# A decoder block on one core: the feed-forward phase put into program order on all engines, its reloads and stores moved

## Chip, core, metric

The kernel runs on one core of a Trainium2 chip. Five engines take part: TensorE (PE, with its weight loads as a row of their own, PEld), VectorE (DVE), ScalarE (ACT), GpSimd (POOL) and SyncE (SP); SP and POOL start the DMAs here. Each engine runs its own list of instructions in order, and waits at an instruction until what it needs from other engines and DMAs is there. The metric is the device time of one execution in microseconds.

## The reference

One layer of a decoder block on 512 tokens of width 2048, all in float32:

```python
h = rmsnorm(x, attn_norm_g)
c_q, c_kv, k_rope, u_pool, gate_logits = split(h @ w_in)
# multi-scale causal pooling of u_pool, latent attention of c_q, c_kv, k_rope
mixed = g_pool * y_pool + g_attn * y_attn
x = x + mixed @ w_out
h2 = rmsnorm(x, ffn_norm_g)
x = x + (silu(h2 @ w_ffn_gate) * (h2 @ w_ffn_up)) @ w_ffn_down
```

w_ffn_gate and w_ffn_up are 2048 x 5632, w_ffn_down is 5632 x 2048. The last two lines are the feed-forward, the only part that the change touches.

## The kernel before

**Accuracy by splitting.** Every float32 operand is used as the sum of two: "hi", a copy rounded to the format in which TensorE is fast (a cast on ACT, L179), and "lo", the rest (a subtraction on DVE, L180: source minus hi). `split` holds both lines. DVE's L180 always waits for ACT's L179 of the same tile.

**Two phases.** The first 1296 us hold the attention and the output projection; they are emitted by a program of their own and the change leaves them alone. The feed-forward follows. It has three kinds of work.

*Blocks* (class `Macro`) compute a 2 x 2 arrangement of products with seven matrix products in place of eight (the scheme of Strassen and Winograd), in the order 1, 5, 6, 2, 7, 3, 4. A product is 8 matmuls of 128x128 by 128x512 with hi (L1090) and 8 by 128x256 with lo (L1093), added into one PSUM bank. Each block loads five weight tiles of 512 KB by SP (L1067), "11", "s1", "12", "s3" and "22"; "s1" and "s3" are sums of two blocks, whose second half is added by an accumulating DMA on POOL (L1069), which waits for the landing of the first half. `prepare(i)` splits the weights of product i: 1 reads "11", 5 "s1", 6 the sum "s1" + "11" written over "11" (DVE, L1075), 2 "12", 7 "s3", 3 the sum "12" + "11" written over "12" (L1077), 4 "22". The split goes into one of five buffers `ws`. `post(i)` works on the result: 1 copies its bank negated into the bank of 6 (ACT), 5 copies its bank to `p5` (ACT, L1108), 6 copies its bank negated into that of 3 (ACT, L1111), 2 and 4 fold a bank into the result tile `gu` (ACT L1099, DVE L1100), 7 adds `p5` to its bank (`w`, DVE L1117), 3 subtracts `p5` from its bank and adds both parts of `w` into `gu` (L1120, L1121). There are two buffers `gu`, one `p5` and one `w`.

- 44 `GateUp` blocks, one for each 128 rows of the hidden layer. They multiply the gate part by the norm's factor (L1151, after product 3), take silu (ACT, L1152), multiply by the up part (L1154, after product 4) and store the 256 KB product to `F_d` in DRAM (SP, L1155).
- 8 `Down` blocks for each half c of the hidden layer. For c = 0 the result is added to `X2_d` in DRAM by an accumulating DMA on POOL (L1174); for c = 1 the block reloads its part of `X2_d` (SP), adds it (L1168) and stores `out` (SP, L1176 after product 3, L1178 after product 4).

*Plain groups* (class `Plain`), 4 ahead of each half of the `Down` blocks, multiply the first 6 of a half's 22 tiles of `F_d` in three passes (24 matmuls a step, 12 steps). Their activations, tiles "ff", are reloaded from `F_d` by POOL and split by `make_act`. At a group's end two results `gu` are added to `X2_d` by POOL (L1213).

*Operands* (class `Operands`): beside the plain groups the other 16 tiles of `F_d` are reloaded by POOL ("t" and "b") and combined on DVE (`difference`, `sums`, with temporaries "d" and "e" in the buffers of `w` and `gu`) and split into the 28 tiles T that the `Down` blocks multiply. The T, raw weight, ff, t, b and xr tiles share a pool of 36 slots.

**What sets the order.** A list of steps (one product of a block, or one step of a plain group) is walked once (L1329 on). At step n the loop first issues the loads that step n + 3 needs and two more, and `prepare` of step n + 3, then the matmuls of step n, then `post` of step n, then what `extra` holds for n (the reloads and operand parts, distributed by `spread`). Only PE keeps that order on its instruction list (L141, `manual_schedule`); the lists of ACT, DVE, POOL and SP are ordered by a scheduler that works from its own estimate of times. A tile's buffer is given back when the last instruction on it is done; one that waits for a buffer waits at its place in its engine's list.

Of the kernel before, what the change touches and what calls it, by code (L numbers as in the profile page):

```python
# [136 lines left out]
def hybrid_block(ctx, tc, xT, pos, wcq, wckv, wkr, wu, wgp, wga, wgrp, wpo, wq, wkv, wao, wo,  # L137
                 wg, wup, wdp, wds, vec, rgain, ident_d, mask_d, freq_d, cnt_d, out):
    nc = tc.nc
    act, dve, pool, pe = nc.scalar, nc.vector, nc.gpsimd, nc.tensor  # L140
# [12 lines left out]
    def slot(dt=F32, name="s"):  # L153
        return slots.tile([128, 2, 512], dt, name=name, tag="s")
# [4 lines left out]
    def tmp(w=512):  # L159
        return work.tile([128, 528], F32, name="tmp", tag="tmp", bufs=6)[:, :w]  # L160
# [15 lines left out]
    def split(hi, lo, src, scale=None):  # L176

        if scale is None:
            act.copy(out=hi, in_=src)  # L179
            dve.tensor_tensor(out=lo, in0=src, in1=hi.bitcast(F32), op=ALU.subtract)  # L180
        else:
            act.activation(out=hi, in_=src, func=AF.Copy, scale=scale)  # L182
            dve.scalar_tensor_tensor(out=lo, in0=src, scalar=scale, in1=hi.bitcast(F32),
                                     op0=ALU.mult, op1=ALU.subtract)
# [103 lines left out]
    def token_sums(o, acc, tag):  # L288

        box = []  # L290

        def run():
            box.append(ps(tag))
            for t in range(NT):
                pe.matmul(box[0][:, 2 * t:2 * t + 2], acc[:, t * 128:(t + 1) * 128], ones[:, 0:2],
                          start=True, stop=True)

        def post():
            dve.tensor_copy(o, box[0][:, 0:2 * NT].rearrange("p (t two) -> p t two", two=2)[:, :, 0])
        return run, post  # L300
# [702 lines left out]
    class Operands:  # L1003
# [9 lines left out]

        def sums(self):
            t, b, d = self.t, self.b, self.d
            e = self.e = self.temp("e")
            dve.tensor_tensor(out=d[:, :, HI], in0=b[:, :, HI], in1=d[:, :, LO], op=ALU.subtract)
            dve.tensor_tensor(out=e[:, :, LO], in0=t[:, :, HI], in1=b[:, :, HI], op=ALU.subtract)
            dve.tensor_tensor(out=e[:, :, HI], in0=b[:, :, LO], in1=d[:, :, HI], op=ALU.subtract)

        def part(self, i):
            src = {1: (self.t, LO), 2: (self.b, LO), 3: (self.b, HI), 5: (self.d, LO)}
            if i in (4, 6, 7):
                src.update({6: (self.d, HI), 7: (self.e, LO), 4: (self.e, HI)})
            r = slot(F32R, "T")
            split(r[:, :, LO], r[:, :, HI], src[i][0][:, :, src[i][1]])
            self.T[i, self.j] = r

        def steps(self):
            return [self.difference, lambda: self.part(1), lambda: self.part(5), self.sums] + \  # L1030
                [lambda i=i: self.part(i) for i in (2, 6, 7, 3, 4)]

    def slot_temp(name):
        return slot(F32, name)
# [5 lines left out]
    acts = {}  # L1040

    def load_acts(dst, f):
        pool.dma_start(dst, F_d[f])

    def make_act(f):
        r = slot(F32R, "ff")
        load_acts(r[:, 1, :].bitcast(F32), f)
        split(r[:, 0, :], r[:, 1, :], r[:, 1, :].bitcast(F32))
        acts[f] = r

    class Macro:

# [73 lines left out]
    fast = [None]  # L1126

    def wide(name):
        return fast[0].tile([128, 2, 512], F32, name=name, tag="w", bufs=1)

    def wide2(name):
        return wide(name) if name == "d" else fast[0].tile([128, 2, 512], F32, name=name, tag="gu", bufs=2)

    def split_unit(src, early=False):

        if early:
            h, l = (slot(F32R, "ws0").rearrange("p a n -> p (a n)") for _ in range(2))
        else:
            r = fast[0].tile([128, 2, 1024], F32R, name="ws", tag="ws", bufs=WS_BUFS)
            h, l = r[:, 0, :], r[:, 1, :]  # L1140
        split(h, l, src)
        return h, l

    class GateUp(Macro):
# [4 lines left out]
        def done(self, i, g):  # L1149
            if i == 3:  # L1150
                dve.tensor_tensor(out=g[:, 0, :], in0=g[:, 0, :], in1=inv2_bc, op=ALU.mult)  # L1151
                act.activation(out=g[:, 0, :], in_=g[:, 0, :], func=AF.Silu)  # L1152
            elif i == 4:
                dve.tensor_tensor(out=g[:, 1, :], in0=g[:, 0, :], in1=g[:, 1, :], op=ALU.mult)  # L1154
                nc.sync.dma_start(F_d[self.f], g[:, 1, :])  # L1155

    class Down(Macro):

# [5 lines left out]
        def done(self, i, g):  # L1164
            if i == 1 and self.last:
                self.x = slot(F32, "xr")
                nc.sync.dma_start(self.x, X2_d[2 * self.j:2 * self.j + 2].rearrange("a p n -> p a n"))
            for a, c in {2: ((0, LO),), 3: ((0, HI), (1, HI)), 4: ((1, LO),)}.get(i, ()):  # L1168
                dve.tensor_tensor(out=g[:, a, c], in0=g[:, a, c], in1=inv2_bc[:, c], op=ALU.mult)
                if self.last:  # L1170
                    dve.tensor_tensor(out=g[:, a, c], in0=g[:, a, c], in1=self.x[:, a, c], op=ALU.add)
            k = 2 * self.j
            if i == 4 and not self.last:
                pool.dma_start(X2_d[k:k + 2].rearrange("a p n -> p a n"), g, accum_op=ALU.add)  # L1174
            elif i == 4:
                nc.sync.dma_start(out[k + 1], g[:, 1, :])  # L1176
            elif i == 3 and self.last:
                nc.sync.dma_start(out[k], g[:, 0, :])  # L1178

    class Plain:  # L1180
# [24 lines left out]
        def post(self, u):  # L1205
            if u < self.nu - 1:
                return
            for a in range(2):
                o = fast[0].tile([128, 2, 512], F32, name="gu", tag="gu", bufs=2)
                for b in range(2):  # L1210
                    dve.tensor_tensor(out=o[:, b, :], in0=self.acc[2 * a + b], in1=inv2_bc, op=ALU.mult)  # L1211
                k = 4 * self.j + 2 * a
                pool.dma_start(X2_d[k:k + 2].rearrange("a p n -> p a n"), o, accum_op=ALU.add)  # L1213

    macros = [GateUp(f) for f in range(FT)]

# [58 lines left out]

    phase = ExitStack()
    fast[0] = phase.enter_context(tc.tile_pool(name="fast", bufs=1, reuse_waits="tile"))

    sums_run, sums_post = token_sums(t42, xacc2[0], "a")
    bc2_prepare, bc2_run = token_bc(inv2_bc, inv2, "a", lambda: fast[0].tile([128, 512], F32, name="dg", tag="gu", bufs=2))  # L1280

    loads, steps, extra = [], [], {}
# [7 lines left out]
    def add_plain(m):  # L1290
        for u in range(m.nu):
            loads.append((m, u))
            steps.append((m, u, len(loads)))

    def spread(first, count, work):

        for n, f in enumerate(work):
            extra.setdefault(first + n * count // len(work), []).append(f)

    def operand_work(key, f0):  # L1300

        r = []
        for j in range(4):
            o = Operands(key, j, None, None, wide2)

            def fetch(o=o, j=j):
                o.t, o.b = slot(F32, "t"), slot(F32, "b")
                for a in range(2):
                    load_acts(o.t[:, a, :], f0 + 2 * j + a)
                    load_acts(o.b[:, a, :], f0 + 8 + 2 * j + a)  # L1310
            r += [fetch] + o.steps()
        return r

    for m in macros:
        add_macro(m)
# [1 line left out]
                  3: [bc2_prepare], 4: [bc2_run]})  # L1317
    for c in range(2):
        f0 = HT * c
        spread(len(steps) - 6, 6, [lambda f=f: make_act(f) for f in range(f0, f0 + 6)])  # L1320
        n = len(steps)
        for j in range(4):
            add_plain(Plain(wdp[c], j, f0, 3, SETS[j % 2]))
        spread(n, 12, operand_work(c, f0 + 6))
        for j in range(8):
            add_macro(Down(c, wds[c], j, c == 1))

    nload, nprep = 2, 2
    for n, (m, i, _) in enumerate(steps):  # L1329
        while nprep < min(len(steps), n + LEAD + 1):  # L1330
            mm, ii, need = steps[nprep]
            while nload < min(len(loads), need + 2):
                loads[nload][0].load(loads[nload][1])
                nload += 1
            mm.prepare(ii)
            nprep += 1
        m.product(i)
        m.post(i)
        for f in extra.get(n, ()):
            f()  # L1340
    phase.close()


# [73 lines left out]
```

## Time and profile before

| | us |
|---|---|
| median of 3 runs | 2649.8 |
| the three runs | 2646.56, 2649.8, 2650.21 |
| the profiled execution | 2645.02 |
| its span, first to last instruction | 2643.0 |
| first phase, gate and up blocks, plain and down | to 1296, to 2126, to 2643 |

The mean granted TensorE clock of the profiled execution is 0.995 of full speed.

How to read the rows of the profile: an instruction row has its start in us, the duration of one, the engine, the line of the kernel, the operation, out<-in by tile names, the tile's shape and type, how many followed directly, and in brackets how long the engine had been idle before it and what it waited for ("<-DVE w L1117": an operation of DVE at L1117 that wrote or read w). "SPq" and "POOLq" are the moments at which a queue gets a DMA. A DMA row has out<-in, the queue, the count, the size of one and the median time from issue to landing. L1090 stands for line 1090 of the kernel before.

### The profile page before, as it was taken

What the parts mean: (1) busy time and instruction counts of PE and PEld (TensorE: products, weight loads), DVE (VectorE), ACT (ScalarE), POOL (GpSimd) and SP (SyncE); (2) the same over time, 40 slices, a digit from 0 to 9 for tenths busy, and PEclk for the clock granted to TensorE, in tenths of its full rate; (3) what the DMA queues carried; (4) which work ended last, traced back from release to release, by engine and by line L of the source; (5) the groups of instructions that cost most, each with busy time, mean ns of one, the idle gap of its engine ahead of it and who ended that gap; (6) DMA issues with size and microseconds to landing.
All of it is one profiled execution on the core that took longest, in us unless ns stands there. A gap on an engine that the chain in (4) does not pass through costs nothing.

```text
span 2643.0 us, 36598 instructions
## 1 busy us (share of the span) xinstructions
PE 2606.7 (99%) x13672; PEld 2236.9 (85%) x13672; DVE 1700.2 (64%) x2828; ACT 1209.8 (46%) x2176; POOL 268.1 (10%) x436
## 2 busy tenths in 40 slices
PE   9999999999999999999999999999999999999999
PEld 7888888888888888888788888888888888887788
DVE  6545332357777744354687777777777786777687
ACT  5224232356676532233455455555555553444343
POOL 0000000013232100000100000000000012112100
PEclk9999999999999999999999999999999999999999
DMA  5223333322222364444587777777777768877885
GB/s 184 92 92 116 112 128 112 124 92 96 92 81 87 113 204 161 132 161 135 181 215 206 196 208 203 191 215 198 195 211 194 211 211 204 213 191 207 211 250 144
DMA packets 140866, 434.17 MB, mean 164 GB/s; under 512 B 15889, under 2 KB 16273, under 8 KB 140689
## 3 DMA queue, kind: packets, MB, share of 16 engines
q1 hardware_dynamic: 112080, 340.60, 37.7%
q0 software_dynamic: 28608, 91.24, 18.8%
q8 instruction: 107, 1.75, 0.3%
q14 instruction: 71, 0.57, 0.1%
HBM read 382.50 MB, written 49.28 MB: 163 GB/s over the span
## 4 chain that ended last, share of the span: by engine, by line
PE 93%; DMA 3%; issue 1%; DVE 1%; ACT 1%; POOL 0%; SPq 0%; POOLq 0%; DVEq 0%; ACTq 0%
PE psa L203 17%; PE psc L203 14%; PE psb L1090 11%; PE psb L203 11%; PE psd L203 8%; PE psa L1090 8%; PE psb L1093 6%; PE psa L1093 4%; PE psd L1090 4%; PE psc L1090 4%; PE psd L1093 2%; PE psc L1093 2%; PE psb L799 1%; DMA ff<-F_d 1%; PE psc L830 1%
## 5 line engine op out<-in xcount | busy, mean ns | idle before, releaser
L180 DVE TENSOR_TENSOR ws<-raw,ws 128x1024 fp32r<-128x1024 f32 x444 | 542.0, 1221 | 241.7 <-ACT ws L179 203.7
L180 DVE TENSOR_TENSOR wsp<-raw,wsp 128x512 fp32r<-128x512 f32 (+2 forms) x426 | 284.5, 673 | 470.7 <-ACT wsp L179 468.4
L179 ACT CAST ws<-raw 128x1024 fp32r<-128x1024 f32 x444 | 465.8, 1050 | 228.9 <-PE psc L1093 95.7
L179 ACT CAST wsp<-raw 128x512 fp32r<-128x512 f32 (+2 forms) x426 | 258.6, 610 | 575.6 <-PE psd L203 279.7
L1090 PE MATMUL psb<-T,ws 128*128 128x512 f32 x1440 | 366.4, 397 | 23.7 <-ACT psc L1111 14.6
L1090 PEld LDWEIGHTS psb<-T,ws 128*128 128x128 f32 x1440 | 261.5, 191 | 72.9 <-ACT psc L1111 15.8
L1090 PE MATMUL psa<-T,ws 128*128 128x512 f32 x960 | 240.6, 392 | 0.0
L203 PE MATMUL psc<-hT,wsp 128*128 128x512 f32 x864 | 228.3, 391 | 0.0
L1093 PEld LDWEIGHTS psb<-T,ws 128*128 128x128 f32 x1440 | 199.4, 193 | 14.5
L1093 PE MATMUL psb<-T,ws 128*128 128x256 f32 x1440 | 203.2, 285 | 0.0
L1090 PEld LDWEIGHTS psa<-T,ws 128*128 128x128 f32 x960 | 173.2, 189 | 31.1
L203 PEld LDWEIGHTS psc<-hT,wsp 128*128 128x128 f32 x864 | 163.1, 189 | 34.2
L203 PE MATMUL psa<-wsp,lr 128*128 128x256 f32 (+1 forms) x1152 | 177.6, 305 | 1.0 <-ACT pt L766 1.0
L203 PEld LDWEIGHTS psa<-wsp,lr 128*128 128x128 f32 x1152 | 163.2, 190 | 4.9 <-ACT pt L766 1.3
L1069 POOL DMA_DIRECT2D raw<-in_wup x88 | 75.1, 854 | 765.8 <-issue 240.1
L203 PE MATMUL psa<-hT,wsp 128*128 128x512 f32 x576 | 148.8, 393 | 3.0 <-ACT hT L182 2.3
L203 PE MATMUL psb<-hT,wsp 128*128 128x512 f32 x576 | 146.9, 390 | 0.0
L1093 PEld LDWEIGHTS psa<-T,ws 128*128 128x128 f32 x960 | 131.0, 190 | 9.4
L1093 PE MATMUL psa<-T,ws 128*128 128x256 f32 x960 | 133.8, 282 | 0.0
L203 PEld LDWEIGHTS psa<-hT,wsp 128*128 128x128 f32 x576 | 108.0, 189 | 27.3 <-ACT hT L182 2.7
L203 PEld LDWEIGHTS psb<-hT,wsp 128*128 128x128 f32 x576 | 107.4, 188 | 21.7
L1090 PE MATMUL psd<-T,ws 128*128 128x512 f32 x480 | 120.3, 392 | 0.5 <-DVE gu L1211 0.5
(268 smaller groups left out, 4010.4 us busy)
## 6 DMA issues: line engine op xcount, KB each, us to landing
raw<-in_wg SPq DMA_DIRECT2D x132, 512.0 KB, 4.5
raw<-in_wup SPq DMA_DIRECT2D x88, 512.0 KB, 4.7
raw<-in_wup POOLq DMA_DIRECT2D x88, 512.0 KB, 5.5
raw<-in_wds SPq DMA_DIRECT2D x80, 512.0 KB, 5.7
raw<-in_wgp SPq DMA_DIRECT2D x32, 512.0 KB, 3.4
raw<-in_wga SPq DMA_DIRECT2D x32, 512.0 KB, 3.4
raw<-in_wao SPq DMA_DIRECT2D x32, 512.0 KB, 3.5
raw<-in_wo SPq DMA_DIRECT2D x32, 512.0 KB, 3.5
```

The lines of the kernel that those rows point to most:

```text
L179: act.copy(out=hi, in_=src)
L180: dve.tensor_tensor(out=lo, in0=src, in1=hi.bitcast(F32), op=ALU.subtract)
L203: pe.matmul(o, w, a, start=first, stop=last, skip_group_check=onto)
L799: pe.matmul(s[:, :w], P.QR[hp, h, q], P.KL[hp, :w], start=False, stop=True)
L830: pe.transpose(box[0][:, j * 128:(j + 1) * 128], P.st[h, i][:, j * 128:(j + 1) * 128], ident)
L1069: pool.dma_start(r, part(*second), accum_op=ALU.add)
L1090: pe.matmul(o, h[:, k * 128:(k + 1) * 128], t[k], start=k == 0 and first, stop=False, skip_group_check=not first)
L1093: pe.matmul(o[:, LO], l[:, k * 128:(k + 1) * 128], t[k][:, LO], start=False, stop=k == HK - 1, skip_group_check=not first)
```

## The change

It does five things, all in the feed-forward:

1. The phase enters `manual_schedule` with all five engines: ACT, DVE, POOL and SP now hold their instructions in the order in which the loop above issues them.
2. `make_act` is cut in two. `load_act`, the reload of an ff tile, is issued 6 and 5 steps ahead of the plain groups (three tiles each); `split_act`, its cast and subtraction, in steps n-3 to n.
3. Stores are put on a list `deferred` and issued after `post` of the step that follows: the store of `F_d` (L1155 before, L1154 after), the accumulations into `X2_d`. The stores of `out` stay where they are.
4. `sums` and `part` work without the temporary "e": the sums are written over parts of "d" and "b" that are no longer read, after part 2 has been made.
5. The reload of operand group j + 1 is issued behind the sums of group j, the first one a step ahead of the plain groups.

The core of the diff:

```diff
         def sums(self):
             t, b, d = self.t, self.b, self.d
-            e = self.e = self.temp("e")
             dve.tensor_tensor(out=d[:, :, HI], in0=b[:, :, HI], in1=d[:, :, LO], op=ALU.subtract)
-            dve.tensor_tensor(out=e[:, :, LO], in0=t[:, :, HI], in1=b[:, :, HI], op=ALU.subtract)
-            dve.tensor_tensor(out=e[:, :, HI], in0=b[:, :, LO], in1=d[:, :, HI], op=ALU.subtract)
+            dve.tensor_tensor(out=d[:, :, LO], in0=t[:, :, HI], in1=b[:, :, HI], op=ALU.subtract)
+            dve.tensor_tensor(out=b[:, :, LO], in0=b[:, :, LO], in1=d[:, :, HI], op=ALU.subtract)
...
-    def make_act(f):
-        r = slot(F32R, "ff")
+    def load_act(f):
+        r = acts[f] = slot(F32R, "ff")
         load_acts(r[:, 1, :].bitcast(F32), f)
+
+    def split_act(f):
+        r = acts[f]
         split(r[:, 0, :], r[:, 1, :], r[:, 1, :].bitcast(F32))
-        acts[f] = r
+
+    deferred = []
...
                 dve.tensor_tensor(out=g[:, 1, :], in0=g[:, 0, :], in1=g[:, 1, :], op=ALU.mult)
-                nc.sync.dma_start(F_d[self.f], g[:, 1, :])
+                deferred.append(lambda: nc.sync.dma_start(F_d[self.f], g[:, 1, :]))
...
             if i == 4 and not self.last:
-                pool.dma_start(X2_d[k:k + 2].rearrange("a p n -> p a n"), g, accum_op=ALU.add)
+                deferred.append(lambda: pool.dma_start(X2_d[k:k + 2].rearrange("a p n -> p a n"), g, accum_op=ALU.add))
...
-                pool.dma_start(X2_d[k:k + 2].rearrange("a p n -> p a n"), o, accum_op=ALU.add)
+                deferred.append(lambda o=o, k=k: pool.dma_start(X2_d[k:k + 2].rearrange("a p n -> p a n"), o, accum_op=ALU.add))
...
+    E = mybir.EngineType
+    phase.enter_context(tc.manual_schedule(engines={E.PE, E.Activation, E.DVE, E.Pool, E.SP}))
...
-        spread(len(steps) - 6, 6, [lambda f=f: make_act(f) for f in range(f0, f0 + 6)])
         n = len(steps)
+        spread(n - 6, 2, [lambda f=f: load_act(f) for f in range(f0, f0 + 6)])
+        spread(n - 3, 4, [lambda f=f: split_act(f) for f in range(f0, f0 + 6)])
         for j in range(4):
             add_plain(Plain(wdp[c], j, f0, 3, SETS[j % 2]))
-        spread(n, 12, operand_work(c, f0 + 6))
+        ahead, work = operand_work(c, f0 + 6)
+        spread(n - 1, 1, ahead)
+        spread(n + 1, 11, work)
...
         m.product(i)
+        late, deferred[:] = deferred[:], []
         m.post(i)
-        for f in extra.get(n, ()):
+        for f in extra.get(n, []) + late:
             f()
+    for f in deferred:
+        f()
```

**SP in the gate and up blocks.** In the rows of the two orders the numbers behind a name tell buffers apart; a block takes 170 of them. Before, raw_15308 and raw_15359 are "s3" and "22" of block 22; raw_15383, 15429, 15455, 15478 and 15529 are "11", "s1", "12", "s3" and "22" of block 23; raw_15553 is "11" of block 24. gu_15111 is the result of block 20, gu_15281 that of block 21.

```order
L1067 DMA raw_15308<-in_wg 128x1024
L1067 DMA raw_15359<-in_wup 128x1024
L1067 DMA raw_15383<-in_wg 128x1024
L1155 DMA F_d_109<-gu_15111 128x512
L1067 DMA raw_15429<-in_wup 128x1024
L1067 DMA raw_15455<-in_wg 128x1024
L1067 DMA raw_15478<-in_wg 128x1024
L1067 DMA raw_15529<-in_wup 128x1024
L1067 DMA raw_15553<-in_wg 128x1024
L1155 DMA F_d_109<-gu_15281 128x512
```

The same place after (lines have moved by two: L1069 is now SP's load, the accumulation on POOL L1071): raw_15113, 15136 and 15186 are "12", "s3" and "22" of block 21; raw_15211, 15257, 15283, 15306 and 15356 are the five loads of block 22; gu_15109 and gu_15279 are the results of blocks 20 and 21.

```order
L1069 DMA raw_15113<-in_wg 128x1024
L1069 DMA raw_15136<-in_wg 128x1024
L1069 DMA raw_15186<-in_wup 128x1024
L1154 DMA F_d_109<-gu_15109 128x512
L1069 DMA raw_15211<-in_wg 128x1024
L1069 DMA raw_15257<-in_wup 128x1024
L1069 DMA raw_15283<-in_wg 128x1024
L1069 DMA raw_15306<-in_wg 128x1024
L1069 DMA raw_15356<-in_wup 128x1024
L1154 DMA F_d_109<-gu_15279 128x512
```

Before, the store of block 20 stood ahead of "s1" of block 23 and behind "11" of that block; after, it stands ahead of "11" and "s1" of block 22.

**DVE at the end of a block.** The rows run from the addition of product 7 to the last product of block 21 (gu_15281 before, gu_15279 after). raw_15259, raw_15213 and raw_15285 are "s1", "11" and "12" of block 22 before, and raw_15308 is its "s3".

```order
L180 TENSOR_TENSOR ws_15311<-raw_15259,ws_15311 128x1024
L1117 TENSOR_TENSOR w_15306<-psb_15211,p5_15235 128x512
L180 TENSOR_TENSOR ws_15335<-raw_15213,ws_15335 128x1024
L1120 TENSOR_TENSOR w_15306<-psc_15257,p5_15235 128x512
L1121 TENSOR_TENSOR gu_15281<-w_15306 128x2x256
L180 TENSOR_TENSOR ws_15361<-raw_15285,ws_15361 128x1024
L1151 TENSOR_TENSOR gu_15281<-gu_15281,bc_110 128x512
L1077 TENSOR_TENSOR raw_15285<-raw_15285,raw_15213 128x1024
L1100 TENSOR_TENSOR gu_15281<-psb_15211,u_15354 128x256
L180 TENSOR_TENSOR ws_15385<-raw_15308,ws_15385 128x1024
L1154 TENSOR_TENSOR gu_15281<-gu_15281 128x512
```

After, raw_15257 and raw_15211 are "s1" and "11" of block 22 (L1077 is now the sum for product 6, L1119 to L1123 the operations of `post`, L1150 and L1153 the two multiplications).

```order
L1119 TENSOR_TENSOR w_15304<-psb_15208,p5_15233 128x512
L180 TENSOR_TENSOR ws_15309<-raw_15257,ws_15309 128x1024
L1122 TENSOR_TENSOR w_15304<-psc_15255,p5_15233 128x512
L1123 TENSOR_TENSOR gu_15279<-w_15304 128x2x256
L1150 TENSOR_TENSOR gu_15279<-gu_15279,bc_110 128x512
L1077 TENSOR_TENSOR raw_15211<-raw_15257,raw_15211 128x1024
L180 TENSOR_TENSOR ws_15333<-raw_15211,ws_15333 128x1024
L1102 TENSOR_TENSOR gu_15279<-psb_15208,u_15352 128x256
L1153 TENSOR_TENSOR gu_15279<-gu_15279 128x512
```

Before, the last multiplication of block 21 stood behind the subtraction for product 7 of block 22; after, it stands behind that for product 6, and the subtraction for product 5 (of raw_15257) has moved behind L1119, into the row of operations that end block 21.

More of the change, by code (lines that the diff above doesn't have):

```diff
@@ L1015, in sums @@
             t, b, d = self.t, self.b, self.d
-            e = self.e = self.temp("e")
             dve.tensor_tensor(out=d[:, :, HI], in0=b[:, :, HI], in1=d[:, :, LO], op=ALU.subtract)
-            dve.tensor_tensor(out=e[:, :, LO], in0=t[:, :, HI], in1=b[:, :, HI], op=ALU.subtract)
-            dve.tensor_tensor(out=e[:, :, HI], in0=b[:, :, LO], in1=d[:, :, HI], op=ALU.subtract)
+            dve.tensor_tensor(out=d[:, :, LO], in0=t[:, :, HI], in1=b[:, :, HI], op=ALU.subtract)
+            dve.tensor_tensor(out=b[:, :, LO], in0=b[:, :, LO], in1=d[:, :, HI], op=ALU.subtract)
         def part(self, i):
-            src = {1: (self.t, LO), 2: (self.b, LO), 3: (self.b, HI), 5: (self.d, LO)}
-            if i in (4, 6, 7):
-                src.update({6: (self.d, HI), 7: (self.e, LO), 4: (self.e, HI)})
+            x, c = {1: (self.t, LO), 5: (self.d, LO), 2: (self.b, LO),
+                    6: (self.d, HI), 7: (self.d, LO), 3: (self.b, HI), 4: (self.b, LO)}[i]
             r = slot(F32R, "T")
-            split(r[:, :, LO], r[:, :, HI], src[i][0][:, :, src[i][1]])
+            split(r[:, :, LO], r[:, :, HI], x[:, :, c])
             self.T[i, self.j] = r
         def steps(self):
-            return [self.difference, lambda: self.part(1), lambda: self.part(5), self.sums] + \
-                [lambda i=i: self.part(i) for i in (2, 6, 7, 3, 4)]
+            return [self.difference] + [lambda i=i: self.part(i) for i in (1, 5, 2)] + [self.sums] + \
+                [lambda i=i: self.part(i) for i in (6, 7, 3, 4)]
     def slot_temp(name):
@@ L1129, in wide @@
         return fast[0].tile([128, 2, 512], F32, name=name, tag="w", bufs=1)
-    def wide2(name):
-        return wide(name) if name == "d" else fast[0].tile([128, 2, 512], F32, name=name, tag="gu", bufs=2)
     def split_unit(src, early=False):
@@ L1300, in operand_work, with fetch @@
     def operand_work(key, f0):
-        r = []
[L1303 to L1312, printed above, removed]
+        os = [Operands(key, j, None, None, wide) for j in range(4)]
+        def fetch(j):
+            o = os[j]
+            o.t, o.b = slot(F32, "t"), slot(F32, "b")
+            for a in range(2):
+                load_acts(o.t[:, a, :], f0 + 2 * j + a)
+                load_acts(o.b[:, a, :], f0 + 8 + 2 * j + a)
+        r = []
+        for j, o in enumerate(os):
+            w = o.steps()
+            if j < 3:
+                w.insert(5, lambda j=j: fetch(j + 1))
+            r += w
+        return [lambda: fetch(0)], r
     for m in macros:
```

## The prediction

> **What bounds the kernel now.** I read the page first, then a table of stages, then PE's timeline in the stages where it idles, then the timelines of ACT, DVE and SP there.
>
> ```profile
> span 2643.0 us, 36598 instructions
> PE 2606.7 (99%) x13672; PEld 2236.9 (85%) x13672; DVE 1700.2 (64%) x2828; ACT 1209.8 (46%) x2176; POOL 268.1 (10%) x436
> ```
>
> PE is busy 2606.7 of 2643.0 us, so at most 36 us of idle time can be won. The table of stages (span, then busy time of PE, PEld, DVE, ACT and POOL with their counts, the granted clock, DMA share, GB/s) tells where the feed-forward holds it:
>
> ```profile
> 1300.00:1400.00 100.00, 94.78 (x540) 82.61 (x539) 76.62 (x91) 52.43 (x69) 12.24 (x14) 1.00 0.84 236
> 1400.00:1500.00 100.00, 100.00 (x575) 88.04 (x574) 75.26 (x84) 50.05 (x67) 9.35 (x11) 1.00 0.76 198
> 2100.00:2200.00 100.00, 98.60 (x519) 84.65 (x518) 78.01 (x99) 52.60 (x74) 15.68 (x24) 1.00 0.71 209
> 2200.00:2300.00 100.00, 95.11 (x492) 81.58 (x491) 71.27 (x92) 39.49 (x52) 19.93 (x22) 0.98 0.84 208
> 2300.00:2400.00 100.00, 91.24 (x504) 79.61 (x503) 67.06 (x83) 46.41 (x62) 16.73 (x21) 0.96 0.79 213
> 2400.00:2500.00 100.00, 94.43 (x438) 79.04 (x437) 73.64 (x102) 39.07 (x54) 21.81 (x26) 0.96 0.78 195
> ```
>
> The gate and up blocks run with PE full (1400 to 1500). The idle time is 5.2 us where the phase opens and 1.4 + 4.9 + 8.8 + 5.6 = 20.7 us around the two plain stages. PE's and ACT's timelines name the causes:
>
> ```profile
> 2153.47 1.16 ACT L179 CAST ff<-ff 128x512 fp32r<-128x512 f32 x2 [4.46 <-DMA ff<-F_d]
> 2253.56 2.60 PE L1090 MATMUL psb<-T,ws 128*128 128x512 f32 x8 [3.71 <-DVE w L1117]
> 2368.90 0.62 ACT L179 CAST ff<-ff 128x512 fp32r<-128x512 f32 x1 [5.81 <-DMA ff<-F_d]
> 2370.06 2.98 PE L1090 MATMUL psb<-T,ws 128*128 128x512 f32 x8 [2.95 <-ACT psc L1111]
> 2394.94 0.62 ACT L179 CAST ff<-ff 128x512 fp32r<-128x512 f32 x1 [5.17 <-DMA ff<-F_d]
> 2397.23 3.78 PE L1090 MATMUL psb<-T,ws 128*128 128x512 f32 x8 [5.81 <-ACT psc L1111]
> 2495.99 3.78 PE L1090 MATMUL psb<-T,ws 128*128 128x512 f32 x8 [4.89 <-DVE w L1117]
> ```
>
> ACT waits at a cast of a reloaded activation, and the bank copy behind it (L1111) comes late to PE. After such a gap eight matmuls take up to 3.78 us, at a lower granted clock.
>
> **What is removed.** The reloads now stand in three groups ahead of their casts, so I take PE's stalls behind the three waits at ff as gone: 1.4 (the stage from 2100) + 2.95 + 5.81 = 10.2 us, and about 3 us of the slow matmuls behind them. The stalls at 2253 and 2495 wait for buffers that X2 stores still hold; I take half of 8.6, 4 us. Together 17, between 0 (the X2 store that is still ahead of the reloads in POOL's queue keeps them late) and 26 (all of it). At the phase's opening I take nothing: POOL's order hardly changes there, and the in-place sums only shift a few 0.69 us operations. Nor do they cost: one slot fewer, one release later, beside a DVE that is busy 64%.
>
> **What is added.** In the gate and up blocks the fixed order moves the store of F_d on SP one block nearer to the loads behind it. Before, the store of block 20 stands ahead of "s1" of block 23; now it stands ahead of "11" and "s1" of block 22. SP waits at the store until DVE has multiplied block 20, and both loads wait with it. On DVE the subtraction that consumes "s1" of block 22 stands ahead of everything that ends block 21, its multiplication included. So store 20 leads to store 21 by a loop that every block must go round once: store, load "s1", the accumulating DMA on POOL, cast, subtraction, the end of block 21, store. If one round takes longer than PE's seven products, the loop sets the pace. PE's round is 2124.91 - 2105.35 = 19.56 us:
>
> ```profile
> 2105.35 2.00 PE L1090 MATMUL psa<-T,ws 128*128 128x512 f32 x8
> 2124.91 2.00 PE L1090 MATMUL psa<-T,ws 128*128 128x512 f32 x8
> 2109.14 0.33 SPq L1155 DMA_DIRECT2D F_d<-gu  x1
> ```
>
> The store stands 3.8 us after its round's start (2109.14).
>
> First piece of the loop, from the store to the landing of "s1". A burst of the same make is in the trace: a store of F_d with loads of 512 KB behind it. Rows are SP's timeline and the landing time of one DMA in a window of its own (of the 2171.50 one, then of the 2172.48 one):
>
> ```profile
> 2170.61 0.33 SPq L1155 DMA_DIRECT2D F_d<-gu  x1
> 2171.50 0.41 SPq L1189 DMA_DIRECT2D raw<-in_wdp  x1
> raw<-in_wdp SPq DMA_DIRECT2D x1, 512.0 KB, 5.1
> 2172.48 0.38 SPq L1189 DMA_DIRECT2D raw<-in_wdp  x1
> raw<-in_wdp SPq DMA_DIRECT2D x1, 512.0 KB, 6.6
> ```
>
> The second load lands 0.89 + 5.1 = 6.0 us after the store's issue, the fourth 1.87 + 6.6 = 8.5.
>
> Second piece, the accumulating DMA: first the median of 40 in the middle of the phase, then three single ones, at 1301.8, 1328.9 and 1309.9, which started beside loads (with a plain load of SP at 1328.6 ahead of the second of them); last, from the chain of waits, the load whose landing the third waited for, and POOL's row for it:
>
> ```profile
> raw<-in_wup POOLq DMA_DIRECT2D x40, 512.0 KB, 5.5
> raw<-in_wup POOLq DMA_DIRECT2D x1, 512.0 KB, 6.0
> raw<-in_wup SPq DMA_DIRECT2D x1, 512.0 KB, 3.7
> raw<-in_wup POOLq DMA_DIRECT2D x1, 512.0 KB, 6.9
> raw<-in_wup POOLq DMA_DIRECT2D x1, 512.0 KB, 8.8
> 1305.28 4.08 DMA raw<-in_wup
> 1309.94 0.87 POOL L1069 DMA_DIRECT2D raw<-in_wup  x1 [7.25 <-DMA raw<-in_wup]
> ```
>
> POOL issues 1309.94 - 1309.36 = 0.6 us after the landing. Now "12", "s3" and "22" are still under way then, as in the single rows; I take 6.5, between 6.0 and 6.9, with 5.5 and 8.8 as ends.
>
> Third piece, from that landing to the next store, on ACT and DVE:
>
> ```profile
> 2119.56 1.05 ACT L179 CAST ws<-raw 128x1024 fp32r<-128x1024 f32 x1 [1.51 <-PE psb L1093]
> 2122.31 0.69 DVE L1120 TENSOR_TENSOR w<-psc,p 128x512 f32<-128x512 f32 x1 [0.44 <-PE psc L1093]
> 2123.04 0.69 DVE L1121 TENSOR_TENSOR gu<-w 128x512 f32<-128x512 f32 x1
> 2123.65 1.22 DVE L180 TENSOR_TENSOR ws<-raw,ws 128x1024 fp32r<-128x1024 f32 x1
> 2124.78 0.68 DVE L1151 TENSOR_TENSOR gu<-gu,bc 128x512 f32<-128x512 f32 x1
> 2125.39 1.22 DVE L1077 TENSOR_TENSOR raw<-raw 128x1024 f32<-128x1024 f32 x1
> 2126.52 0.42 DVE L1100 TENSOR_TENSOR gu<-psb,u 128x256 f32<-128x256 f32 x1
> 2126.85 1.21 DVE L180 TENSOR_TENSOR ws<-raw,ws 128x1024 fp32r<-128x1024 f32 x1
> 2127.99 0.68 DVE L1154 TENSOR_TENSOR gu<-gu 128x512 f32<-128x512 f32 x1
> ```
>
> The loop holds these eight DVE operations (2122.31 to 2128.67, 6.4 us) and two casts of 1.05 that DVE waits for (products 5 and 6), 2.1; I add 0.5 for six handovers without overlap. That is 9.0 us.
>
> The round: 6.0 + 0.6 + 6.5 + 9.0 = 22.1, 2.5 us over 19.56. There are 42 such rounds (stores 0 to 41 with loads behind them). The operand of product 6 has 4 us in hand at first: product 3 ends 6/7 of a round after the block's start, 16.8, the three operations behind it, L1077 and the cast take 4.4, and product 6 of the next block starts at 19.6 + 2 x 2.8 = 25.1. So 42 x 2.5 - 4 = 101 us. With 5.5 for the accumulation it is 1.5 a round, 59 us; with 8.8 it is 4.8, 198 us. PE meanwhile idles a little in each block; slow matmuls after such gaps lie inside its waiting.
>
> The second half of the down blocks has the same loop through the stores of the result on SP, which hold back "22", the reload of x, "11" and "s1": "s1" lands with the fourth 512 KB transfer, at 8.5, and four more operations of about 0.4 us, less one of 0.68, make the third piece 10.1. The round is 8.5 + 0.6 + 6.5 + 10.1 = 25.7, 6.1 over, six times, less 4: 33 us (27 to 46 with 5.5 and 8.8). In the first half the store is an X2 accumulation on POOL, ahead of that of "s1":
>
> ```profile
> X_d<-gu POOLq DMA_DIRECT2D x24, 512.0 KB, 9.8
> ```
>
> The loads are not behind it; 9.8 + 9.0 = 18.8 is under 19.56. I take nothing, with 18 us (3 a block) as the other end, when "s1" lands a third of a transfer later.
>
> Sum against the profiled execution of 2645.0 us (span 2643.0, and 2.0 around it): 2645 + 101 + 33 - 17 = 2762. That execution is 4.8 below the median of 2649.8 and 1.5 below the fastest of the three, 2646.56; so much is inside the range.
>
> The Trainium skill speaks for a shorter loop: "DMA: Bandwidth & Descriptors", section "Anatomy of one DMA — SWDGE (gpsimd) path", fits a DMA at 2.0 us plus its bytes at 436 GB/s, an estimate of 3.2 us for 512 KB. By it "s1" would land at 2.0 + 0.6 + 1.2 + 1.2 = 5.0 after the store and its accumulation 3.2 later, the round would be 17.8, and the sum 2645 - 17 = 2628. The trace differs: 40 accumulations of 512 KB have a median of 5.5.
>
> **Rivals.** First, faster: the loop is too short to bind. For it: "s1" behind a small store could land at 4.6 (0.9 + 3.7, the load's first part without company), its accumulation at 5.5 without company, so 4.6 + 0.6 + 5.5 + 9.0 = 19.7, hardly over PE's round. Then only the removed stalls count, also in the down blocks: 2628. Against it: "11" and the store are ahead of "s1" in one queue, and the burst's row says 6.0. It decides at 10.6 us from store to landed accumulation. Chance 0.11. The Trainium skill's fit ("DMA: Bandwidth & Descriptors", as above) gives this case.
>
> Second, the loop binds only in the last down blocks, where two more transfers are ahead: 2645 - 17 + 27 = 2655, or 2646 with all 26 of the stalls gone. Chance 0.03.
>
> Third, slower still: every accumulation meets traffic as at 1309.9 (8.8), and the first down half binds too: 2645 + 198 + 46 + 18 - 17 = 2890. For it: all five loads of a block now start within 3 us. Against it: at 1309.9 three more loads started behind it; now none do. Chance 0.08.
>
> **The numbers.** The forecast, a loop that sets the pace, has 0.78: 2762, with 2645 + 59 + 27 - 26 = 2705 to about 2890 as its own bounds. I give 2690 to 2890, which leaves out the first two rivals and the top of the third. Under 0.2% (5 us, about what a measurement of this kernel can tell) I see 0.02, most of the second rival; faster 0.11, slower 0.87.
>
> **What would show it.** Right: in the stages from 1400 to 2100 PE busy falls to 85 to 92%, equal blocks start about 22 us apart, PE's gaps stand at product 6 (released by ACT's cast, ws) and product 7 (by the bank copy), ACT waits for the DMA of raw (in_wup), SP at the store for DVE, and DMA comes in bursts. The ff waits on ACT are gone. Wrong: PE stays at 100% there; or blocks stay 19.6 us apart with "s1" landing before the cast needs it; or the time is lost around the plain stages instead.

## The result, and the profile after

| | before | after |
|---|---|---|
| median | 2648.5 us | 2768.5 us |
| range, runs | 2646.6 to 2650.2, 4 | 2760.9 to 2774.3, 4 |
| ratio | | 1.045 [1.042, 1.049] |
| span of the profiled execution | 2643.0 us | 2759.0 us |

The change costs 120 us; forecast were 2762 us and a loop through the store of F_d. The page of after:

```profile
span 2759.0 us, 36565 instructions
PE 2644.8 (96%) x13672; PEld 2260.0 (82%) x13672; DVE 1706.9 (62%) x2828; ACT 1193.8 (43%) x2176; POOL 268.7 (10%) x436
```

PE does the same 13672 matmuls. Its idle time grew from 36 to 114 us, and its busy time by 38 us: matmuls behind a gap run slowly. The table of stages (columns as in the prediction):

```profile
1400.00:1500.00 100.00, 92.53 (x511) 80.57 (x510) 65.42 (x72) 43.35 (x58) 8.53 (x10) 0.97 0.66 194
2400.00:2500.00 100.00, 97.63 (x550) 85.15 (x549) 75.52 (x95) 47.18 (x65) 19.80 (x27) 1.00 0.86 235
```

The picture is turned round: the gate and up blocks, full before, now have PE at 92.5. The work in which before lost 8.8 us (2300 to 2400 there) comes about 96 us later in after, and loses 2.4. The waits of SP name the change, first before, then after (us in all, times, longest):

```profile
SPq L1155 <- DVE gu L1154: 27.4, 43, 17.6
```

```profile
SPq L1154 <- DVE gu L1153: 822.7, 44, 20.5
```

SP waited 27 us for the products that it stores; now it is 823 us, 18.7 in each block, and the loads stand behind. The chain of waits in order of time shows one round of the loop (start, us, what; pieces of a few hundredths are left out). It begins at the landing of an accumulation and ends where the next one starts:

```profile
1803.92 1.06 ACT ws L179
...
1805.01 1.23 DVE ws L180
1806.23 0.61 DVE w L1122
...
1806.87 0.70 DVE gu L1123
...
1807.59 0.69 DVE gu L1150
1808.28 1.15 DVE raw L1077
...
1809.53 1.06 ACT ws L179
...
1810.61 1.23 DVE ws L180
1811.84 0.35 DVE gu L1102
...
1812.21 0.70 DVE gu L1153
1812.93 0.33 SPq L1154
...
1813.82 5.35 DMA raw<-in_wup
...
1819.73 3.33 DMA raw<-in_wup
```

That is the forecast's loop, operation by operation: cast and subtraction of "s1", the operations that end the block, the store, behind it the load of "s1" (landed 6.2 us after the store), then the accumulation (its 3.33 us are cut by the window; the row of this DMA gives 6.5). No piece of PE is in it. PE shows the loop only as a gap at product 6, with slow matmuls behind it (PE's and ACT's timelines):

```profile
1834.67 3.52 PE L1092 MATMUL psb<-T,ws 128*128 128x512 f32 x8 [2.47 <-ACT psb L1107]
```

```profile
1831.87 1.05 ACT L179 CAST ws<-raw 128x1024 fp32r<-128x1024 f32 x1 [0.58 <-DVE raw L1077]
1832.82 0.37 ACT L1101 COPY u<-psb 128x256 f32<-128x256 f32 x1
1833.08 1.05 ACT L179 CAST ws<-raw 128x1024 fp32r<-128x1024 f32 x1
1834.03 0.59 ACT L1107 ACTIVATE psb<-psa 128x512 f32<-128x512 f32 x1
```

Where the time went is read from the starts of product 5 in both timelines of PE (block 1, block 43, second block of the last down half; before, then after):

```profile
1325.32 2.00 PE L1090 MATMUL psd<-T,ws 128*128 128x512 f32 x8
2147.28 2.00 PE L1090 MATMUL psd<-T,ws 128*128 128x512 f32 x8
2503.84 2.00 PE L1090 MATMUL psd<-T,ws 128*128 128x512 f32 x8
```

```profile
1332.28 2.00 PE L1092 MATMUL psd<-T,ws 128*128 128x512 f32 x8
2247.26 2.00 PE L1092 MATMUL psd<-T,ws 128*128 128x512 f32 x8
2581.99 2.00 PE L1092 MATMUL psd<-T,ws 128*128 128x512 f32 x8
```

Up to block 1 after loses 7.0 us. The 42 rounds to block 43 take 915.0 in place of 822.0: 93.0 lost. From there to the second block of the last down half it is 334.7 in place of 356.6: 21.8 won. From there to the end 177.0 in place of 139.2: 37.9 lost. 7.0 + 93.0 - 21.8 + 37.9 = 116, the difference of the two profiled executions; that of after is the fastest of its four, 7.6 under their median.

### The profile page after: what moved, and what is told of

It reads as the page before. It is cut to its first block, busy times and chain, and to the rows that moved or that the text cites. A ratio compares the mean times of both kernels' runs of the same rounds, so it can differ in the third digit from the quotient of the medians.

```text
span 2759.0 us, 36565 instructions
## 1 busy us (share of the span) xinstructions
PE 2644.8 (96%) x13672; PEld 2260.0 (82%) x13672; DVE 1706.9 (62%) x2828; ACT 1193.8 (43%) x2176; POOL 268.7 (10%) x436
## 4 chain that ended last, share of the span: by engine, by line
PE 55%; issue 18%; DMA 15%; DVE 8%; ACT 3%; SPq 1%; POOL 0%; POOLq 0%; ACTq 0%; DVEq 0%
PE psa L203 16%; PE psc L203 14%; DMA raw<-in_wup 11%; PE psb L203 11%; PE psd L203 8%; DMA raw<-in_wds 3%; DVE ws L180 3%; ACT ws L179 2%; PE psb L1092 1%; DVE raw L1077 1%; PE psb L799 1%; DVE gu L1123 1%; PE psa L1092 1%; PE psc L830 1%; PE psb L1095 1%
## 5 line engine op out<-in xcount | busy, mean ns | idle before, releaser
L1092 PE MATMUL psb<-T,ws 128*128 128x512 f32 x1440 | 390.9, 416 | 100.0 <-ACT psb L1107 94.5
L1092 PEld LDWEIGHTS psb<-T,ws 128*128 128x128 f32 x1440 | 272.0, 199 | 161.8 <-ACT psb L1107 104.6
L1095 PEld LDWEIGHTS psb<-T,ws 128*128 128x128 f32 x1440 | 205.1, 198 | 15.9
L1071 POOL DMA_DIRECT2D raw<-in_wup x88 | 75.3, 859 | 869.5 <-DVE ws L180 507.7
L203 PEld LDWEIGHTS psb<-hT,wsp 128*128 128x128 f32 x576 | 107.3, 188 | 21.8
L1092 PE MATMUL psc<-T,ws 128*128 128x512 f32 x480 | 120.6, 393 | 0.0
```

Of the source, the lines that this page charges most:

```text
L203: pe.matmul(o, w, a, start=first, stop=last, skip_group_check=onto)
L1071: pool.dma_start(r, part(*second), accum_op=ALU.add)
L1092: pe.matmul(o, h[:, k * 128:(k + 1) * 128], t[k], start=k == 0 and first, stop=False, skip_group_check=not first)
L1095: pe.matmul(o[:, LO], l[:, k * 128:(k + 1) * 128], t[k][:, LO], start=False, stop=k == HK - 1, skip_group_check=not first)
```

## The experiments

All ratios are against the kernel before, run on the same chip. A round is read from one row of SP's view, the first and last of 44 stores divided by 43; after it is (2271.8 - 1334.5) / 43 = 21.8 us:

```profile
L1154 SPq DMA_DIRECT2D F_d<-gu x44: 326/326/327, 1334.5 to 2271.8; - x44
```

**Cut the loop at the store.** `deferred` gets a step number with each store; the accumulations into `X2_d` keep their delay of 1.

```diff
-                deferred.append(lambda: nc.sync.dma_start(F_d[self.f], g[:, 1, :]))
+                defer(4, lambda: nc.sync.dma_start(F_d[self.f], g[:, 1, :]))
```

> The store of F_d is issued four products late in place of one, so that on SP the loads 11 and s1 of block b+2 stand ahead of the store of block b; nothing else changes. The loop theory: store b no longer holds back s1, the loop is cut in the gate and up blocks, their rounds fall from 21.9 to 19.56 us and PE wins back the 93 us that it lost between block 1 and block 43; the opening (+7) and the last down blocks (+38) stay: 2768 - 93 = 2675 us. The rival, that the fixed order of ACT and DVE itself (a bank copy behind casts) starves PE: the rounds stay above 21 us and the time above 2740.

Measured: 2663.3 us, ratio 1.005 [1.003, 1.006]. The row of the store:

```profile
L1157 SPq DMA_DIRECT2D F_d<-gu x44: 326/326/327, 1335.9 to 2174.8; - x44
```

The round is 19.5 us, with ACT and DVE in the same fixed order. The time is 12 us under the expectation; 7.6 of them because the 93 us of the profiled execution were taken off the median. The loss of these blocks was the place of one store on SP, and the rival is out.

**Move "s1" nearer to the store.**

```diff
-    LOADS = ("11", "s1", "12", "s3", "22")
+    LOADS = ("s1", "11", "12", "s3", "22")
```

> The loads of a block are issued as s1, 11, 12, s3, 22 in place of 11, s1, 12, s3, 22. The loop theory: s1 lands as the first load behind the store, at about 4.3 us (0.4 + 3.9) in place of 6.0, so the round shrinks by 1.7 to 20.2 us, 42 x 1.7 = 71 us; in the last down blocks s1 moves from fourth to third place, 6 x 0.8 = 5 us: 2768 - 76 = 2692 us, up to 2735 if the accumulation, which then starts among more loads, takes 7.4 us as its slowest ones did. The rival, a fixed order that starves PE whatever SP does: no change, 2768 within 10.

Measured: 2770.6 us, 1.046 [1.044, 1.047]: no change clear of the noise. The theory's expectation failed; the number is the rival's, but its reason had fallen with the run before. The chain shows the round with its store, load and accumulation:

```profile
1818.82 0.33 SPq L1154
...
1819.20 3.81 DMA raw<-in_wup
...
1823.57 7.57 DMA raw<-in_wup
```

"s1" did land early, 4.2 us behind the store, but its accumulation, started early, took 7.57. On the mean of 42 rounds (in each the store, the landing of "s1", issue and landing of its accumulation, and the next store, taken from the trace) "s1" landed at 4.4 in place of 6.0, and the accumulation took 8.1 in place of 6.25; it was complete 13.0 us behind the store, 12.8 before. So the two terms aren't independent, and a second reading came up: the five loads are served together with the accumulation, and the burst as a whole sets when it is complete.

**The store in its old place.** In the changed kernel its delay becomes 0 (1 there, 4 in the first experiment).

> The store of F_d is issued behind its own product, as it was written before the change, not one product late; all engines stay in program order. On SP the store of block b then stands ahead of 22 of block b+1 as well as 11 and s1 of block b+2. The loop theory: s1 lands as the third load behind the store, 0.85 us later, so the round grows to 22.7 us: 42 x 0.85 = 36 us more, 2804 us. The rival, that issuing stores late is what costs: the time falls towards that of the kernel before, under 2700.

Measured: 2782.6 us, 1.051 [1.049, 1.053]. The sign is the theory's, the size 14 in place of 36 us: "s1" lands 1.2 us later (7.2), but its accumulation then runs in 5.6, complete at 13.3. The same trade again.

**A smaller burst.** In the kernel that loads "s1" first, the gate and up blocks load three tiles in place of five. The run leaves out the weights of "12" and "22", so it computes something else in the same number of operations.

```diff
+        def load(self, name):
+            if name in ("s1", "11", "s3"):
+                super().load(name)
...
+            src = raw[{1: "11", 6: "11", 2: "11", 7: "s3", 5: "s1", 4: "s3", 3: "s3"}[i]]
```

> As the kernel that loads s1 first (2770.6 us, with the loop at 22.1 us a round), but the gate and up blocks load only s1, 11 and s3; products 2 and 3 and 4 take their weights from tiles that are there, with the same casts, subtractions and sums. It leaves out the weights of 12 and 22, so two of the five loads. There the accumulation of s1 took 8.1 us when it started 4.4 us behind the store, and 6.25 when it started 6.0 behind: I read this as the burst of five loads being served as a whole, so that s1 is complete about 13 us after the store wherever it stands. With three loads it should take 5.9, as beside two loads of the kernel before: round 4.4 + 0.55 + 5.9 + 9.1 = 19.95, 2770 - 42 x 2.1 = 2683 us, with 2675 as the floor where PE sets the pace. The rival, that the early accumulation is slow for another reason than the loads behind it: 2770 within 15.

Measured: 2679.5 us, 1.012 [1.011, 1.014]. The accumulations in the stage from 1400 to 2100 (median of the DMAs, first with "s1" first and five loads, then with three):

```profile
raw<-in_wup POOLq DMA_DIRECT2D x64, 512.0 KB, 7.5
```

```profile
raw<-in_wup POOLq DMA_DIRECT2D x68, 512.0 KB, 6.0
```

The early accumulation was slow for the loads beside it: without two of them the round falls from 22.1 to 20.2 us, as expected. The Trainium skill ("DMA: Bandwidth & Descriptors", section "Issuing engines are not separate DMA queues") says that DMAs of all issuing engines run on the same 16 DMA engines and interleave; these runs agree, 8.1, 6.25 and 5.6 us for the same 512 KB as ever less of the burst is left beside it.

**ACT and DVE left to the scheduler.**

```diff
-    phase.enter_context(tc.manual_schedule(engines={E.PE, E.Activation, E.DVE, E.Pool, E.SP}))
+    phase.enter_context(tc.manual_schedule(engines={E.PE, E.Pool, E.SP}))
```

> Only PE, POOL and SP stand in program order; the scheduler orders ACT and DVE. Its order puts L1077 ahead of the subtraction of s1 and the subtractions of products 2 and 7 between that and the block's last multiplication. The loop theory: store, s1 and accumulation stay; the third piece of the loop becomes the sum of the DVE operations from the landing to the multiplication, about 11.2 us in place of 9.1, so the round is 24.0 us: 42 x 2.1 = 88 us more, 2856 us, and somewhat more with the last down blocks. The rival, that the fixed order of ACT and DVE starves PE: faster, under 2740.

Measured: 2843.1 us, 1.073 [1.072, 1.075], on the theory's side by sign; that the size agrees is luck. In the profiled execution (against that of after) the 42 rounds lose 53.7 us where 88 were expected, the stretch from there to the second block of the last down half loses 63, and the opening and the end win 7 and 27. From landing to store it is 10.3 us on the mean of the rounds, not 11.2, and the chain goes on from L1119 through matmuls of PE, so this loop isn't one of DVE alone. What it shows is that the fixed order of ACT and DVE does not cost the 120 us; the scheduler's order is 75 us worse behind the same store.

**Both stores out of the way.** F_d and `out` are stored four products late.

> The stores of F_d and those of out are issued four products late; the rest is the changed kernel. The loop theory: the last down blocks lose their loop too (38 us in the changed kernel, 35 in the one with only F_d late), and only the removed stalls and the opening are left: 2663 - 35 = 2628 us, 20 us under the kernel before. The rival, that the last down blocks are slow for their fixed order or for the reload of x: above 2650 us.

Measured: 2633.7 us, 0.995 [0.994, 0.997], faster than both kernels. From product 5 of their second block to the end, the last down blocks lost 35 us in the first experiment and 4 here: their loop was that of the stores of `out`. 6 us are missing to the expected 2628; in the profiled execution the opening lost 9.5 us to block 2 in place of 6.6.

**Bank copies ahead of casts.** In the kernel with all stores late, the product and `post` of a step are issued before the loads and casts for later steps.

> As the kernel with all stores late, but in each step the work on the product's result is issued ahead of the casts for the product three steps on, so that on ACT a bank copy no longer stands behind a cast that waits for a load or a sum. If the 6.5 us that the opening loses come from that place (product 2 waits there for the copy L1107, behind the cast of product 6), 3 to 6 us come back: 2628 - 5 = 2623 us. If they come from the loads that wait for slots, no change: 2628 within 2.

Measured: 2660.9 us, 1.005 [1.004, 1.007]: a miss. It kept the opening's loss (6.2 us to block 1) and made a new one, a gap at each product 6 of the gate and up blocks:

```profile
1355.39 2.12 PE L1095 MATMUL psb<-T,ws 128*128 128x512 f32 x8 [0.54 <-ACT psb L1110]
```

The row of ACT ahead of that copy (L1107, here L1110; the sum for product 6 is L1080):

```profile
1353.80 1.05 ACT L179 CAST ws<-raw 128x1024 fp32r<-128x1024 f32 x1 [3.27 <-DVE raw L1080]
1354.76 0.58 ACT L1110 ACTIVATE psb<-psa 128x512 f32<-128x512 f32 x1
```

The copy still stands behind the cast of product 6, and the sum that this cast waits for now stands on DVE behind the operations that end the block before. The rounds are 20.4 us, and what was to come back at the opening did not: PE's gap at product 2 of block 0 is gone, but the one at product 7 (copy L1113, here L1116) grew to 7.9 us. That copy too stands behind a cast that waits for a sum on DVE.

**The opening.** In the kernel with all stores late, ACT and DVE are left to the scheduler for block 0 alone.

```diff
-    phase.enter_context(tc.manual_schedule(engines={E.PE, E.Activation, E.DVE, E.Pool, E.SP}))
+    phase.enter_context(tc.manual_schedule(engines={E.PE, E.Pool, E.SP}))
...
     for n, (m, i, _) in enumerate(steps):
+        if n == 7:
+            phase.enter_context(tc.manual_schedule(engines={E.PE, E.Activation, E.DVE, E.Pool, E.SP}))
```

> As the kernel with all stores late, but for the first seven steps (block 0) ACT and DVE are ordered by the scheduler, and in program order only from block 1 on. In the run with ACT and DVE free throughout, block 1 began as early as before the change, so the 6.5 to 9.5 us that the opening loses belong to the fixed order of these two. If so they come back: 2634 - 7 = 2627 us. The rival, that POOL's or SP's fixed order holds the loads of block 1 back: 2634 within 2.

Measured: 2626.1 us, 0.992 [0.991, 0.994], the fastest of all. PE's waits at the opening of after, and where product 5 of block 1 stands in this run:

```profile
1305.33 3.29 PE L1092 MATMUL psa<-T,ws 128*128 128x512 f32 x8 [2.99 <-ACT psb L1107]
...
1317.77 3.78 PE L1092 MATMUL psb<-T,ws 128*128 128x512 f32 x8 [4.14 <-ACT psc L1113]
```

```profile
1324.04 2.00 PE L1095 MATMUL psd<-T,ws 128*128 128x512 f32 x8
```

1324.0 in place of 1332.3 (1331.6 with all stores late): the opening's loss is the fixed order of ACT and DVE in block 0. In the trace of after, the two copies that PE waits for (L1107 at 1304.70, L1113 at 1317.13) stand on ACT behind casts that wait, through a sum on DVE, for loads that landed at 1300.1 and 1309.7.

**The lead of the reloads.** With all stores late, `load_act` and `split_act` are issued together again:

```diff
-        spread(n - 6, 2, [lambda f=f: load_act(f) for f in range(f0, f0 + 6)])
-        spread(n - 3, 4, [lambda f=f: split_act(f) for f in range(f0, f0 + 6)])
+        spread(n - 6, 6, [lambda f=f: [load_act(f), split_act(f)] for f in range(f0, f0 + 6)])
```

> As the kernel with all stores late, but each reload of an ff tile is issued together with its cast and subtraction again, one per step from n-6 on, as before the change. If the gain around the plain groups comes from reloads that are issued ahead of their casts, the stalls of ACT at ff come back, 10 us of PE idle and 3 us of slow matmuls: 2628 + 13 = 2641 us. The rival, that the gain comes from the fixed order (no scheduler placing the casts ahead of bank copies) or from the late X2 stores: 2628 within 4.

Measured: 2643.6 us, 0.999 [0.998, 1.000]: 10 us of the gain are the lead. ACT's waits at the casts of ff, before and after the change:

```profile
ACT ff L179 <- DMA ff<-F_d: 21.7, 6, 5.8
```

```profile
ACT ff L179 <- DMA ff<-F_d: 2.2, 2, 1.4
```

**The lead alone**, in the kernel before, with its scheduler:

> The kernel before, with only the reloads of ff issued two to five steps ahead of their casts; ACT, DVE, POOL and SP stay with the scheduler. If a lead in the program is enough, 10 to 13 us of the stalls at ff go: 2647 - 12 = 2635 us. If the scheduler sets the place of reloads and casts itself, and the lead only counts where the order is kept: 2647 within 3.

Measured: 2645.8 us, 0.999 [0.998, 1.000]. At most a few us: the lead counts where the order is kept.

**The X2 stores** issued right behind their product, all others late:

> As the kernel with all stores late, but the accumulations into X2 (plain groups and first down blocks) are issued right behind their product again. Between block 43 and block 53 the kernel with late stores and a lead won 27 us on the one before, the one with late stores and no lead 11. If these 11 us come from the late X2 stores, the kernel loses them: 2634 + 9 = 2643 us; in the prediction I had put 4 us on them, 2638. The rival, that they come from the order or from the sums in place: 2634 within 3.

Measured: 2632.5 us, 0.995 [0.993, 0.996], 1.2 under the kernel with all stores late: no gain from the late X2 stores is seen. The four runs scatter by 7 us, and from block 43 to the second block of the last down half the profiled execution wins 23.3 in place of 26.8, so a few us stay possible; the 11 are out.

**The sums with their temporary**, in the buffers of `gu`, all stores late:

```diff
-            dve.tensor_tensor(out=d[:, :, LO], in0=t[:, :, HI], in1=b[:, :, HI], op=ALU.subtract)
-            dve.tensor_tensor(out=b[:, :, LO], in0=b[:, :, LO], in1=d[:, :, HI], op=ALU.subtract)
+            e = self.e = self.temp("e")
+            dve.tensor_tensor(out=e[:, :, LO], in0=t[:, :, HI], in1=b[:, :, HI], op=ALU.subtract)
+            dve.tensor_tensor(out=e[:, :, HI], in0=b[:, :, LO], in1=d[:, :, HI], op=ALU.subtract)
...
+    def wide2(name):
+        return wide(name) if name == "d" else fast[0].tile([128, 2, 512], F32, name=name, tag="gu", bufs=2)
...
```

> As the kernel with all stores late, but the operand sums use the temporary e again, in the buffers of gu. The prediction put nothing on the sums in place: 2634 within 3. The rival: e keeps a buffer gu from the plain results until part 4 is split, the waits for w and gu of the kernel before come back, 2634 + 8 = 2642 us.

Measured: 2670.6 us, 1.009 [1.008, 1.011], 37 us slower than with the sums in place. Its DVE timeline around the first plain groups:

```profile
2192.27 1.29 DVE L1218 TENSOR_TENSOR gu<-psc,bc 128x512 f32<-128x512 f32 x2 [6.49 <-DMA X_d<-gu]
2200.31 0.69 DVE L1018 TENSOR_TENSOR e<-t,b 128x512 f32<-128x512 f32 x1 [6.16 <-DMA X_d<-gu]
...
2219.38 0.69 DVE L1218 TENSOR_TENSOR gu<-psc,bc 128x512 f32<-128x512 f32 x1 [6.54 <-DMA X_d<-gu]
...
2239.74 1.29 DVE L1218 TENSOR_TENSOR gu<-psc,bc 128x512 f32<-128x512 f32 x2 [7.85 <-DMA X_d<-gu]
...
2259.29 0.69 DVE L1218 TENSOR_TENSOR gu<-psc,bc 128x512 f32<-128x512 f32 x1 [6.44 <-DMA X_d<-gu]
```

Plain results, block results and e share two buffers, and in program order each waits for an X2 store to land with all of DVE behind it; PE then waits up to 12 us:

```profile
2260.72 3.75 PE L1097 MATMUL psd<-T,ws 128*128 128x512 f32 x8 [11.97 <-DVE gu L1218]
```

## Why the prediction was right, and where it wasn't

**The loop.** The mechanism, its place and its size held. Store to "s1" 6.0, handover 0.6, accumulation 6.5, landing to store 9.0 were forecast; the means of the 42 rounds are 6.0, 0.54, 6.25 and 9.1, together 21.9 where 22.1 was said. 101 us were put on it, 93 it cost in the profiled execution. The first rival (too short to bind) needed 10.6 us from store to landed accumulation; it was 12.8, and the rival is out. The estimate of 17.8 for the round, worked out from the Trainium skill's fit ("DMA: Bandwidth & Descriptors", section "Anatomy of one DMA — SWDGE (gpsimd) path"), uses it for SP's loads too, though that section is about DMAs of GpSimd, and has 3.2 us for the accumulation. Company is not all that it lacks: the accumulation that POOL started at 1275.0 in the kernel before had no other DMA beside it and took 5.4. What was luck is that the two DMA terms were right one by one: taken as independent they misled about both changes of the order, "s1" as first load and the store in its old place.

**The last down blocks.** 33 us forecast, 37.9 measured. A round of it, from SP's timeline and the chain (in between "s1", issued at 2637.51, landed after 6.6):

```profile
2635.58 0.34 SPq L1175 DMA_DIRECT2D out<-gu  x1
```

```profile
2644.65 5.64 DMA raw<-in_wds
...
2660.54 0.34 SPq L1175
```

The accumulation starts 9.1 us behind the store (8.5 + 0.6 were forecast) and takes 5.6, and from its landing to the next store it is 10.2; the round is 25.0 where 25.7 was said (25.4 on the mean of six, from the stores at 2585.75 and 2737.92). The prediction's 10.1 for the last piece adds up to 10.0. The chain names an operation of DVE as what released this accumulation; "s1" landed at the same time, 0.6 ahead of it, as ahead of the others. With the stores late 4 us of the 37.9 are left.

**The first down blocks.** Nothing forecast, nothing to speak of measured: five rounds, from 2355.72 to 2454.52, are 1.0 us longer than before.

**The removed stalls.** 17 forecast, 21.8 measured, but two of its steps do not hold as they stand. "I take half of 8.6, 4 us" for the late X2 stores: no run shows a gain from them. And of the in-place sums "nor do they cost" was true and half the story: in program order the temporary would cost 37 us, since it takes a buffer of `gu` that X2 stores hold. The wait for a buffer that an X2 store holds was seen rightly; what removes most of it is one user fewer of that buffer, not the later store. What the sums in place would be worth in the kernel before, under its scheduler, wasn't tried.

**The opening.** "At the phase's opening I take nothing, POOL's order hardly changes there": 7.0 us were lost, to the order of ACT and DVE, which that step didn't look at. It and the loop's 8 us too many nearly cancel, and so do the 4.9 too few of the last down blocks and the 4.8 too few of the stalls, which is why the sum (116 against 117) looks better than its terms. That is luck.

**The signs.** The gap at product 6 was forecast as released by the cast; it is released by the bank copy L1107 that the fixed order puts 2.2 us behind that cast. The gap at product 7 didn't come. PE busy was put at 85 to 92%; the stages from 1400 to 2100 show 90.6 to 93.6, since slow matmuls count as busy. Rounds of about 22 us, SP's wait at the store and the end of the waits at ff came as forecast.

## What to carry to other kernels

A store on the queue that also issues loads is a wait for the result, and every load behind it inherits that wait; follow it round, since a store that holds back a load that holds back the next store sets a pace of its own. Price such a round by when the whole burst behind the store is served, and expect little from moving a load within it; move the store behind the loads instead. Where an order is fixed by hand, look for buffers with a third user and for copies that stand behind casts of late loads: the scheduler's order had softened both.

## What the hardware showed that was not expected

An accumulating DMA of 512 KB took 5.4 us where it ran alone (at 1275.0 in the kernel before), but behind a store its time depends on the loads beside it: it took 5.6, 6.25 or 8.1 us as it began 7.7, 6.5 or 5.0 us behind the store that opens a burst of five loads, and was complete after 13.3, 12.8 and 13.0. Starting it 2.7 us earlier gained 0.3.
